# Two blocks of gated features turned by TensorE in the first feed-forward step of a decoder trunk

## The chip, the cores and the metric

The kernel runs on one core of one Trainium2 chip. The metric is device time in microseconds for one execution, as the median of several runs. A core has five engines with a queue each: TensorE (PE in the rows, its weight loads PEld), VectorE (DVE), ScalarE (ACT), GpSimd (POOL) and SyncE (SP), which here issues nearly all DMA transfers and does nothing else.

## The reference

The reference is a decoder trunk of two layers on 256 tokens of width 1024, in float32. Each layer has a feed-forward half step, a mixing step with two kinds of attention, a second feed-forward half step and a gated input embedding. The change touches only the first feed-forward half step of the first layer:

```
def swiglu(x, w_gate, w_up, w_down):
    return (jax.nn.silu(x @ w_gate) * (x @ w_up)) @ w_down

h = h + 0.5 * swiglu(rms_norm(h, ffn1_norm), ffn1_w_gate, ffn1_w_up, ffn1_w_down)
```

The hidden width is 2816. The product of `silu(gate)` and `up` is called the gated features below. `w_down` contracts over them, so they have to stand with features on the partitions, while the matmuls that make them leave tokens on the partitions. Somewhere between they are turned.

## The kernel before

**Operands in two parts.** Every matmul of weights is done as three (`mm3`, lines 250 to 256): each operand is split into a high half, rounded for TensorE, and a low half that holds the rest. For a weight tile of 128x1024, `Unit.load` (line 141) issues one DMA of 512 KB into `raw` (line 148, on SyncE), then ScalarE makes the high half `wh` (line 152) and VectorE the low half `wl` (line 153). `raw` has 7 buffers and the pair `wh`, `wl` has 8. So each weight tile costs VectorE and ScalarE one pass, beside the matmuls that use it.

**The feed-forward step** (`ffn`, line 531) goes through six blocks of 512 hidden features (the last has 256). An ordinary block runs the gate matmuls `g` and then the up matmuls `u` for two groups of 128 tokens, 48 matmuls each, from eight weight tiles. In a *wide seven* block (`wide_seven`, line 573) the gate and up matmuls of the first half of the contraction are one 2x2 block product by seven multiplications: `Seven.operands_own_first` loads four raw tiles, VectorE forms sums of them (line 188), and seven operand pairs are made (`Seven.parts`, lines 193 and 194). Such a block has fewer matmuls and more work for VectorE. In the first step of the program only block 3 is of this kind; in all other steps blocks 1 and 3 are. Block 0 of the first step runs its gate and up matmuls interleaved while inputs still arrive, and its gating is done only behind the gate matmuls of block 1, when the norm of the input is known.

**Gating and turning.** `gated` (line 534) lets ScalarE make `silu` of `g` (tile `s`, line 536) and then VectorE the gated features `pr` from `u` and `s` (line 540). `Gates.add` (line 495) turns them: VectorE transposes each 32x32 square of `pr` in place (line 502), SyncE writes `pr` to memory as `m` (line 504, 256 KB), four more transfers of 64 KB bring it back in another order as `ft` (line 509), and then `parts` (line 511) splits `ft` into the halves `fh` by ScalarE (line 516) and `fl` by VectorE (line 517). Blocks 1 to 3 need sums of the features as well (`Gates.sums`, lines 469 to 472 and 476 to 481), because the down product is again done by seven multiplications. The columns of the gate and up weights are put into a fitting order on the host (`turned_order`), so that the features come back in the right place.

**The order of the work.** Python emits the instructions, and a planner then orders each engine's queue by the sequence of emission and by when it expects inputs and buffers to be there. Once the program is built, each queue is fixed and runs strictly in its order. `soon(us, f)` and `tick` place pieces of work so many microseconds of estimated TensorE time later in the emission: `back` (the transfers of `ft`) 2.5 us and `parts` 7 or 8 us after `add`. `after(later, earlier)` fixes the order of two instructions on the same engine. PSUM has eight banks, all in one pool.

Of the kernel before, what the change touches and what calls it, by code (L numbers as in the profile page):

```python
# [9 lines left out]
F32 = mybir.dt.float32  # L10
F32R = mybir.dt.float32r
BF16 = mybir.dt.bfloat16
AF = mybir.ActivationFunctionType
ALU = mybir.AluOpType
# [3 lines left out]
P = 128  # L18
# [13 lines left out]
SEVEN = (1, 2, 3)  # L32

BACK, PARTS = 2.5, 7.0


def turned_order(n):


    import numpy as np

    return np.arange(n).reshape(n // P, 4, 32).transpose(1, 0, 2).reshape(-1)


def wide_sevens(first):

    return (3,) if first else (1, 3)
# [15 lines left out]
def trunk(ctx: ExitStack, tc: tile.TileContext, xT, xr, pT, w, gains, fgain, consts, out):  # L65
    nc = tc.nc
# [34 lines left out]
    ident = c_sb[:, 0:P]  # L101
# [12 lines left out]
    def after(later, earlier):  # L114

        tc.add_manual_dep(later.ins, earlier.ins.name, mybir.DependencyInfo(mybir.DependencyClass.NoSync, mybir.DependencyReason.DATA), reason="order")
# [9 lines left out]
    newest_load, newest_wh = [None], [None]  # L126
    fence = [None, None]

    class Unit:


        def __init__(self, nk, cols=None, sub=1, cut=1, again=None):
            self.u = at[0] if again is None else again.u
            at[0] += again is None
            self.cols = cols or UNIT // nk
            self.per = max(1, PIECE // self.cols)
            self.sub, self.cut = sub, cut
            self.parts, self.here = {}, set()
# [97 lines left out]
    def soon(us, f):  # L236
        due.append((pe[0] + us, len(due), f))
# [14 lines left out]
    newest_mm = [None]  # L252
# [8 lines left out]
    def both(x, *ix):  # L261
        return tuple(t[ix] for t in x)
# [32 lines left out]
    def in_runs(x):  # L295

        return x.rearrange("p j (a s) -> p j a s", s=32)
# [134 lines left out]
    class Gates:  # L432


        def __init__(self, tag):
            self.tag, self.f, self.s, self.turned = tag, {}, {}, {}

        def tile(self, i):
            if i not in self.f:
# [12 lines left out]
        def sums(self, i):  # L452

            a, b = self.turned[i, 0], self.turned[i, 1]
            lo, hi = (slice(None), slice(0, 2)), (slice(None), slice(2, 4))
            e = SEVEN.index(i)
            if e == 0:

                self.spare = tuple(x_p.tile([P, KC, T], F32R, tag=f"x{q}", name=f"sx{q}_{self.tag}") for q in "hl")
            if e < 2:  # L460
                homes = [[q[:, 4 * e + k].rearrange("p (a b) -> p a b", a=2) for q in self.spare] for k in range(4)]
            else:

                homes = [[q[:, 2 + k].rearrange("p (a b) -> p a b", a=2) for q in self.tile(NBLK - 1)] for k in range(2)]
                homes += [[q[:, 0:2, P:T] for q in self.tile(c)] for c in SEVEN[:2]]
            two = [wt("w3", f"sum{k}_{self.tag}_{i}") for k in range(2)]
            ss = [two[k // 2][:, k % 2].rearrange("p (a b) -> p a b", a=2) for k in range(4)]
            s1, s2, s3, s4 = (in_runs(s) for s in ss)
            nc.vector.tensor_tensor(s1, b[lo], b[hi], ALU.subtract)
            nc.vector.tensor_tensor(s2, s1, a[lo], ALU.subtract)  # L470
            nc.vector.tensor_tensor(s3, a[lo], b[lo], ALU.subtract)
            nc.vector.tensor_tensor(s4, s2, a[hi], ALU.add)
            if e < 2:
                for k in range(2):
                    sh, sl = (q[:, 4 * e + 2 * k : 4 * e + 2 * k + 2] for q in self.spare)
                    nc.scalar.activation(sh, two[k], AF.Copy)
                    nc.vector.tensor_tensor(sl, two[k], sh.bitcast(F32), ALU.subtract)
            else:
                for k, (sh, sl) in zip(ss, homes):
                    nc.scalar.activation(sh, k, AF.Copy)  # L480
                    nc.vector.tensor_tensor(sl, k, sh.bitcast(F32), ALU.subtract)
            self.s[i] = homes
# [13 lines left out]
        def add(self, i, t, pr, more):  # L496


            f = self.block(i)
            n = 4 if i < NBLK - 1 else 2  # L500
            name = f"{self.tag}_{i}{t}"
            nc.vector.transpose(pr, pr)
            m = mem_p.tile([P, 4, n * 32], F32, tag="turn", name=f"m_{name}")
            nc.sync.dma_start(m, pr.rearrange("p (q r) -> p q r", q=4))
            a = wt("w2", f"ft_{name}", 4, n * 32)

            def back():
                for q in range(4):
                    nc.sync.dma_start(a[32 * q : 32 * q + 32], m[:, q].rearrange("(a f) r -> f a r", a=4))

            def parts():
                self.turned[i, t] = v = a.rearrange("p a (j s) -> p j a s", j=n)

                ks = slice(2 if i in SEVEN and t else 0, n)
                fh, fl = (in_runs(q) for q in both(f, slice(None), ks, slice(t * P, (t + 1) * P)))
                after(nc.scalar.activation(fh, v[:, ks], AF.Copy), newest_wh[0])
                nc.vector.tensor_tensor(fl, v[:, ks], fh.bitcast(F32), ALU.subtract)
                if i in SEVEN and t:
                    self.sums(i)

            soon(BACK, back)
            soon(PARTS + t, parts)

    def seven_mm(banks, x_of, ops, first, last):

# [3 lines left out]
                mm3(banks[p], x_of(p, j), (wh[:, c], wl[:, c]), first(p) and j == 0, last(p) and j == 1, skip_group_check=True)  # L529

    def ffn(x, n, tag, gcol, between=None, feed=None):
        gates = Gates(tag)

        def gated(i, t, g, u, m=512):
            s = flat("w0", f"s_{tag}_{i}{t}")[:, :m]
# [71 lines left out]
        for i in range(NBLK):  # L607
# [18 lines left out]
            if i == 0 and feed:  # L626
# [7 lines left out]
                first = [g, u]  # L634
# [38 lines left out]
        p = {2: d[0][0], 3: d[0][1], 4: d[1][0]}  # L673
# [16 lines left out]
        u, v, a, b = (flat(f"w{k}", f"{m}7_{tag}") for k, m in enumerate("uvab"))  # L690
# [376 lines left out]
    n = Norm("in")  # L1067
# [18 lines left out]
    for L in range(DEPTH):  # L1086
        g0 = L * G_LAYER
        x, n = ffn(x, n, f"a{L}", g0 + G_MIX, feed=None if L else start)
        x, n = mix(x, n, L, g0)
# [12 lines left out]
def _weights(i):  # L1102

    import numpy as np

    def cols(w, m):

        return w[:, m].reshape(-1, P, len(m)).transpose(1, 0, 2).reshape(P, -1)

    ar = np.arange  # L1110
    units = []
    for L in range(DEPTH):

        def wide(w, m):

            units.extend(cols(w[k : k + 512], m) for k in range(0, DM, 512))

        def ffn(n):
            wg, wu, wd = (i[f"{n}_w_{s}"][L] for s in ("gate", "up", "down"))
            for j in range(NBLK - 1):  # L1120
                m = 512 * j + turned_order(512)
                if j in wide_sevens(L == 0 and n == "ffn1"):
                    units.extend(np.concatenate([cols(v[k : k + 256], m) for v in (wg, wu)], axis=1) for k in (0, 256))
                    units.extend(cols(v[512:], m) for v in (wg, wu))
                    continue
                wide(wg, m)
                wide(wu, m)
            m = DFF - 256 + turned_order(256)
            wide(np.concatenate([wg[:, m], wu[:, m]], axis=1), ar(512))

            def down(b):
                units.extend(cols(wd[k : k + 256], ar(DM)) for k in range(512 * b, min(512 * b + 512, DFF), 256))

            def seven(b):
                for k in (512 * b, 512 * b + 256):
                    units.append(np.concatenate([cols(wd[k : k + 256], ar(c, c + 512)) for c in (0, 512)], axis=1))

            down(0)
            down(NBLK - 1)
            for b in SEVEN:  # L1140
                seven(b)
            down(4)

        ffn("ffn1")
        wi = i["w_in"][L]
        rot = np.r_[32:64, 0:32]
        wide(wi, ar(1024, 1536))
        for m in (0, 512, 256, 768):
            units.append(cols(wi, ar(m, m + 256)))
        units.append(cols(wi, ar(1536, 1792)))  # L1150
        units.append(cols(wi, np.r_[1792:1920, 1920:1984, 1920 + rot]))
        uq = i["w_uq"][L]
        nope = np.concatenate([192 * h + ar(128) for h in range(4)])
        rope = np.concatenate([192 * h + 128 + ar(64) for h in range(4)])
        rotd = np.concatenate([192 * h + 128 + rot for h in range(4)])
        units.append(cols(uq, np.r_[nope, rope, rotd]))
        ukv = i["w_ukv"][L]
        kn = np.concatenate([256 * h + ar(128) for h in range(4)])
        u = np.zeros((P, UNIT), ukv.dtype)
        u[:, :1024] = cols(ukv, np.r_[kn, kn + 128])  # L1160
        units.append(u)
        for k in range(0, DM, 256):
            units.append(cols(i["w_out"][L][k : k + 256], ar(DM)))
        ffn("ffn2")
        units.append(cols(i["w_ple_proj"][L], ar(DM)))
        for m in range(0, DM, 512):
            wide(i["w_ple_gate"][L], ar(m, m + 512))
    return np.stack(units)
# [55 lines left out]
```

## Time and profile before

| | us |
|---|---|
| median of 3 runs | 1006.04 |
| lowest and highest run | 1004.79, 1007.29 |
| profiled execution | 1003.63 |
| its span, first to last instruction | 1001.8 |
| TensorE busy in the span | 981.6 |
| VectorE busy | 861.9 |
| ScalarE busy | 635.7 |

The profile is of one execution. Times in it count from the first instruction. A busy share is an average over a millisecond; where a change works on a short stretch, the table of that stretch counts, above all the number of matmuls that started in it. A matmul's recorded length overlaps with the next, so the spacing of starts tells the rate. A wait names the instruction that came last.

### The profile page before, as it was taken

The page shows a single profiled execution, that of the slowest core. Times are in us where ns is not written, and L with a number is a line of the kernel's source. Part 1 is how long each engine was busy: PE and PEld are TensorE (multiplying, and loading weights), DVE is VectorE, ACT ScalarE, POOL GpSimd, SP SyncE. Part 2 cuts the span into 40 slices and gives each one's busy share as a digit, 9 for nine tenths or more (in the row PEclk, how much of TensorE's full clock was granted, in tenths as well). Part 3 has the DMA queues.
Part 4 walks back from the last instruction along what each step waited for, and adds up shares of the span by engine and source line. Part 5 has one row for each costly group of instructions (what it writes and reads, how often), then busy time and mean ns, then how long its engine had stood idle before and what let it go on. Part 6 is the DMA issues. An engine that isn't in the chain of part 4 may idle for free.

```text
span 1001.8 us, 14087 instructions
## 1 busy us (share of the span) xinstructions
PE 981.6 (98%) x4888; PEld 824.2 (82%) x4888; DVE 861.9 (86%) x1218; ACT 635.7 (63%) x974; POOL 12.4 (1%) x13
## 2 busy tenths in 40 slices
PE   9998999999999999999999999999999999999996
PEld 7875888899888888887788888888998888888875
DVE  6689999967679999799998998899676799989995
ACT  6746656848566566567676556567766755756664
POOL 0000000000100000000000000002000000000000
PEclk9999999999999999999999999999999999999999
DMA  8876875675233778685737686676733357776651
GB/s 302 302 252 202 302 231 188 230 257 175 98 127 108 268 224 274 197 259 194 262 105 264 229 272 213 212 249 210 274 106 106 126 174 251 267 240 204 222 187 43
DMA packets 88055, 210.50 MB, mean 210 GB/s; under 512 B 14000, under 2 KB 35632, under 8 KB 87984
## 3 DMA queue, kind: packets, MB, share of 16 engines
q1 hardware_dynamic: 87552, 209.03, 62.1%
q8 instruction: 38, 0.62, 0.2%
q10 hardware_dynamic: 432, 0.57, 0.2%
q14 instruction: 33, 0.27, 0.1%
HBM read 196.98 MB, written 12.58 MB: 209 GB/s over the span
## 4 chain that ended last, share of the span: by engine, by line
PE 86%; DVE 5%; DMA 4%; ACT 3%; issue 1%; SPq 0%; ACTq 0%; DVEq 0%
DMA raw<-in_w 4%; PE p_b L256 3%; PE g_a L256 3%; PE p_b L257 3%; PE g_a L258 3%; PE g_a L257 3%; PE g_b L257 3%; PE g_b L258 3%; PE g_b L256 3%; PE p_b L258 3%; PE d_a L257 3%; PE d_a L258 3%; PE d_a L256 3%; PE p_a L257 3%; PE p_a L258 3%; PE p_a L256 2%
## 5 line engine op out<-in xcount | busy, mean ns | idle before, releaser
L153 DVE TENSOR_TENSOR wl<-raw,wh 128x1024 fp32r<-128x1024 f32 (+1 forms) x278 | 321.0, 1187 | 49.5 <-ACT wh L152 48.1
L152 ACT ACTIVATE wh<-raw 128x1024 fp32r<-128x1024 f32 (+1 forms) x278 | 278.5, 1031 | 103.2 <-DMA raw<-in_w 47.4
L193 ACT ACTIVATE wh<-raw 128x1024 fp32r<-128x1024 f32 x133 | 139.0, 1058 | 130.0 <-DVE raw L188 98.9
L194 DVE TENSOR_TENSOR wl<-raw,wh 128x1024 fp32r<-128x1024 f32 x133 | 159.4, 1216 | 11.1 <-ACT wh L193 10.4
L188 DVE TENSOR_TENSOR raw<-raw,raw 128x1024 f32<-128x1024 f32 x76 | 92.6, 1220 | 4.5 <-DMA raw<-in_w 2.4
L256 PE MATMUL d_a<-wh,fh_a 128*128 128x512 f32 x108 | 42.3, 391 | 0.0
L258 PE MATMUL d_b<-wh,fl_b 128*128 128x512 f32 x108 | 42.2, 391 | 0.0
L256 PE MATMUL d_b<-wh,fh_b 128*128 128x512 f32 x108 | 42.2, 391 | 0.0
L258 PE MATMUL d_a<-wh,fl_a 128*128 128x512 f32 x108 | 42.1, 390 | 0.0
L257 PE MATMUL d_b<-wl,fh_b 128*128 128x512 f32 x108 | 42.1, 389 | 0.0
L257 PE MATMUL d_a<-wl,fh_a 128*128 128x512 f32 x108 | 42.0, 389 | 0.0
L256 PE MATMUL g_a<-wh,x0h 128*128 128x512 f32 x80 | 31.1, 390 | 0.3 <-ACT x0h L305 0.3
L257 PE MATMUL g_a<-wl,x0h 128*128 128x512 f32 x80 | 31.0, 389 | 0.0
L258 PE MATMUL g_a<-wh,x0l 128*128 128x512 f32 x80 | 31.0, 389 | 0.0
L257 PE MATMUL u_a<-wl,x0h 128*128 128x512 f32 x64 | 25.2, 394 | 0.5 <-DVE wl L153 0.5
L256 PE MATMUL g_b<-wh,x_mix0h 128*128 128x512 f32 x64 | 25.1, 392 | 0.0
L256 PE MATMUL g_b<-wh,x_mix1h 128*128 128x512 f32 x64 | 25.1, 392 | 0.0
L256 PE MATMUL g_a<-wh,xe0h 128*128 128x512 f32 x64 | 25.0, 391 | 0.0
L258 PE MATMUL u_a<-wh,x0l 128*128 128x512 f32 x64 | 25.0, 390 | 0.0
L258 PE MATMUL g_a<-wh,xe0l 128*128 128x512 f32 x64 | 24.9, 390 | 0.0
L257 PE MATMUL g_a<-wl,xe0h 128*128 128x512 f32 x64 | 24.9, 389 | 0.0
L258 PE MATMUL g_b<-wh,x_mix0l 128*128 128x512 f32 x64 | 24.9, 389 | 0.0
(552 smaller groups left out, 2683.9 us busy)
## 6 DMA issues: line engine op xcount, KB each, us to landing
raw<-in_w SPq DMA_DIRECT2D x338, 512.0 KB, 5.1
m_a<-pr_a SPq DMA_DIRECT2D x20, 256.0 KB, 2.1
ft_a<-m_a SPq DMA_DIRECT2D x80, 64.0 KB, 2.7
m_b<-pr_b SPq DMA_DIRECT2D x20, 256.0 KB, 2.3
ft_b<-m_b SPq DMA_DIRECT2D x80, 64.0 KB, 2.9
raw<-in_w SPq DMA_DIRECT2D x16, 256.0 KB, 4.4
xin<-in_xT SPq DMA_DIRECT2D x4, 256.0 KB, 4.7
h<-in_xr SPq DMA_DIRECT2D x2, 512.0 KB, 8.0
```

Source lines behind the costliest of these rows:

```text
L152: nc.scalar.activation(wh[:, a], r[:, a], AF.Copy),
L153: nc.vector.tensor_tensor(wl[:, a], r[:, a], wh[:, a].bitcast(F32), ALU.subtract),
L188: nc.vector.tensor_tensor(self.raw[o], self.raw[a], self.raw[b], op)
L193: newest_wh[0] = nc.scalar.activation(wh, r, AF.Copy)
L194: nc.vector.tensor_tensor(wl, r, wh.bitcast(F32), ALU.subtract)
L256: nc.tensor.matmul(o, ah, bh, start=start, stop=False, **kw)
L257: nc.tensor.matmul(o, ah, bl, start=False, stop=False, **kw)
L258: newest_mm[0] = nc.tensor.matmul(o, al, bh, start=False, stop=stop, **kw)
```

## The change

In the first feed-forward step blocks 0 and 1 no longer pass through VectorE's transposes and memory. TensorE turns each 128x128 square of `pr` with the identity into a PSUM bank, four squares for each block and group of tokens, and `parts` reads the bank. As an instruction here takes one operand from PSUM where two would be needed, `sums` first copies one quarter of `b` by ScalarE. `soon` places the transposes: for block 1, 1.3 and 2.2 us of estimated TensorE time behind its gating, for block 0 another 4.5 us later. The weight columns of these two blocks keep their natural order. Blocks 2 to 5 of the step, and all other steps, stay as they are. For them `after` is called behind `parts` in place of within it.

```
+def moved(first, i):
+    return not first or i > 1
...
-        def __init__(self, tag):
-            self.tag, self.f, self.s, self.turned = tag, {}, {}, {}
+        def __init__(self, tag, first):
+            self.tag, self.first, self.f, self.s, self.turned = tag, first, {}, {}, {}
...
-            nc.vector.tensor_tensor(s1, b[lo], b[hi], ALU.subtract)
+            blo = b[lo]
+            if not moved(self.first, i):
+                blo = s3
+                nc.scalar.copy(s3, b[lo])
+            nc.vector.tensor_tensor(s1, blo, b[hi], ALU.subtract)
             nc.vector.tensor_tensor(s2, s1, a[lo], ALU.subtract)
-            nc.vector.tensor_tensor(s3, a[lo], b[lo], ALU.subtract)
+            nc.vector.tensor_tensor(s3, a[lo], blo, ALU.subtract)
             nc.vector.tensor_tensor(s4, s2, a[hi], ALU.add)
...
             name = f"{self.tag}_{i}{t}"
+
+            def parts(v):
+                self.turned[i, t] = v
+                ks = slice(2 if i in SEVEN and t else 0, n)
+                fh, fl = (in_runs(q) for q in both(f, slice(None), ks, slice(t * P, (t + 1) * P)))
+                h1 = nc.scalar.activation(fh, v[:, ks], AF.Copy)
+                nc.vector.tensor_tensor(fl, v[:, ks], fh.bitcast(F32), ALU.subtract)
+                if i in SEVEN and t:
+                    self.sums(i)
+                return h1
+
+            if not moved(self.first, i):
+                def go():
+                    a = bank(f"ft_{name}")[:, : n * P]
+                    behind = newest_mm[0]
+                    for j in range(n):
+                        after(nc.tensor.transpose(a[:, j * P : (j + 1) * P], pr[:, j * P : (j + 1) * P], ident), behind)
+                    parts(in_runs(a.rearrange("p (a b) -> p a b", a=n)))
+
+                soon(1.3 + 0.9 * t + more, go)
+                return
             nc.vector.transpose(pr, pr)
             m = mem_p.tile([P, 4, n * 32], F32, tag="turn", name=f"m_{name}")
             nc.sync.dma_start(m, pr.rearrange("p (q r) -> p q r", q=4))
...
             soon(BACK, back)
-            soon(PARTS + t, parts)
+            soon(PARTS + t, lambda: after(parts(a.rearrange("p a (j s) -> p j a s", j=n)), newest_wh[0]))
...
-        gates = Gates(tag)
+        gates = Gates(tag, feed is not None)
...
+                first = L == 0 and n == "ffn1"
-                m = 512 * j + turned_order(512)
+                m = 512 * j + (turned_order(512) if moved(first, j) else ar(512))
```

## Rows read from the trace of the kernel before

**Rows 1.** The page: TensorE's row of the forty slices, busy tenths of 25 us each.
```profile
PE   9998999999999999999999999999999999999996
```

**Rows 2.** The table by stretches. Columns: stretch in us, its length, then busy us and the number of instructions of PE, PEld, DVE, ACT and POOL, the granted clock of TensorE as a share of full speed, the DMA share and GB/s. The last stretch lies in the second feed-forward step.
```profile
40.00:60.00 20.00, 20.00 (x90) 16.57 (x89) 12.12 (x14) 7.85 (x9) 0.00 (x0) 1.00 0.67 206
60.00:80.00 20.00, 16.97 (x66) 12.38 (x64) 19.16 (x28) 11.65 (x17) 0.00 (x0) 0.91 0.78 281
80.00:100.00 20.00, 16.90 (x69) 12.75 (x70) 19.90 (x25) 14.20 (x17) 0.00 (x0) 1.00 0.65 208
100.00:120.00 20.00, 20.00 (x89) 16.55 (x89) 17.61 (x24) 12.50 (x17) 0.00 (x0) 1.00 0.89 294
310.00:330.00 20.00, 20.00 (x90) 16.56 (x89) 19.97 (x23) 13.51 (x16) 0.00 (x0) 1.00 0.39 130
```

**Rows 3.** The waits of TensorE in 60:95, each with its total in us, the number of times and the longest; the longest three totals.
```profile
PE p_a L257 <- DVE wl L194: 3.8, 3, 2.0
PE p_a L256 <- ACT wh L193: 1.6, 2, 1.1
PE u_a L257 <- DVE wl L153: 0.5, 1, 0.5
```

**Rows 4.** The timeline of SyncE's issues: start, time of the group of issues, line, what is moved, and how many.
```profile
22.84 5.32 SPq L148 DMA_DIRECT2D raw<-in_w  x5
37.46 0.92 SPq L504 DMA_DIRECT2D m_a<-pr_a  x2
...
39.52 4.15 SPq L509 DMA_DIRECT2D ft_a<-m_a  x8
43.77 1.32 SPq L148 DMA_DIRECT2D raw<-in_w  x3
51.94 1.14 SPq L504 DMA_DIRECT2D m_a<-pr_a  x2
53.19 0.38 SPq L148 DMA_DIRECT2D raw<-in_w  x1
54.02 5.59 SPq L509 DMA_DIRECT2D ft_a<-m_a  x8
```

**Rows 5.** Waits again, in the same form: SyncE's in 28:76, ScalarE's and VectorE's in 36:66.
```profile
SPq L504 <- DVE pr_a L502: 21.6, 5, 8.4
...
ACT wh L152 <- DMA raw<-in_w: 11.6, 4, 8.4
...
DVE wl L153 <- ACT wh L152: 4.6, 1, 4.6
DVE pr_a L540 <- PE u_a L258: 3.0, 1, 3.0
...
DVE wl L153 <- PE u_a L258: 0.8, 1, 0.8
```

**Rows 6.** The timeline of VectorE in 28:95: start, time, line and operation, how many, and in brackets the idle time before and what ended it.
```profile
36.73 1.29 DVE L502 STREAM_TRANSPOSE pr_a<-pr_a 128x512 f32<-128x512 f32 x2
...
49.26 1.43 DVE L540 SCALAR_TENSOR_TENSOR pr_a<-u_a,hr_in,s_a 128x512 f32<-128x512 f32 x2 [2.97 <-PE u_a L258]
...
60.49 1.23 DVE L153 TENSOR_TENSOR wl<-raw,wh 128x1024 fp32r<-128x1024 f32 x1 [4.60 <-ACT wh L152]
...
65.90 2.35 DVE L153 TENSOR_TENSOR wl<-raw,wh 128x1024 fp32r<-128x1024 f32 x2
...
75.19 1.18 DVE L194 TENSOR_TENSOR wl<-raw,wh 128x1024 fp32r<-128x1024 f32 x1
```

**Rows 7.** Where the seven products start on TensorE, first in the first step (tile p_a), then in the second (tile p_b), with count, shortest, median and longest ns, and the first and last start; and between them the table by stretches for line 194 alone, over the 35.6 us ahead of each start: stretch, length, busy us and number of VectorE's instructions on that line, granted clock, DMA share, GB/s.
```profile
L256 PE MATMUL p_a<-wh,x0h x17: 389/389/502, 72.3 to 99.2; 128*128 128x512 f32 x17
...
36.70:72.30 35.60, 1.22 (x1) 1.00 0.75 249
284.70:320.30 35.60, 6.01 (x5) 1.00 0.31 100
...
L256 PE MATMUL p_b<-wh,x_mix0h x36: 389/389/496, 320.7 to 382.0; 128*128 128x512 f32 x36
```

**Rows 8.** The timeline of TensorE in 185:193, where transposes of h stand between matmuls, and the same transposes as a group of the tile xt_a (shortest, median and longest ns, first and last start).
```profile
185.97 0.39 PE L258 MATMUL d_a<-wh,fl_a 128*128 128x512 f32 x1
186.20 0.60 PE L371 MATMUL xt_a<-c_sb,h 128*128 128x128 f32 x4
186.56 0.48 PE L256 MATMUL d_a<-wh,fh_a 128*128 128x512 f32 x1
186.87 0.40 PE L257 MATMUL d_a<-wl,fh_a 128*128 128x512 f32 x1
...
L371 PE MATMUL xt_a<-c_sb,h x32: 270/272/273, 186.2 to 683.3; 128*128 128x128 f32 x32
```

**Rows 9.** Single operations by their sources: VectorE with one operand from a PSUM bank (p_a), ScalarE's copy from such a bank, and VectorE from SBUF (ft_a).
```profile
L587 DVE TENSOR_TENSOR ch_a<-ch_a,p_a x1: 678/678/678, 84.0 to 84.0; 128x512 f32<-128x512 f32 x1
L584 ACT COPY ch_a<-p_a x1: 586/586/586, 73.9 to 73.9; 128x512 f32<-128x512 f32 x1
...
L517 DVE TENSOR_TENSOR fl_a<-ft_a,fh_a x6: 416/682/684, 45.6 to 87.1; 128x512 fp32r<-128x512 f32 x4, 128x256 fp32r<-128x256 f32 x2
```

**Rows 10.** The chain of work that ended last, in 0:140: start, time, what. Two matmuls: the first of u of block 1, and the first that used the low half of the tile behind the seven products.
```profile
38.76 0.45 PE u_a L256 x2
...
91.77 0.50 PE p_a L257
```

More of the change, by code (lines that the diff above doesn't have):

```diff
@@ L509, in back @@
                     nc.sync.dma_start(a[32 * q : 32 * q + 32], m[:, q].rearrange("(a f) r -> f a r", a=4))
[L511 to L519, printed above, removed]
             soon(BACK, back)
-            soon(PARTS + t, parts)
+            soon(PARTS + t, lambda: after(parts(a.rearrange("p a (j s) -> p j a s", j=n)), newest_wh[0]))
     def seven_mm(banks, x_of, ops, first, last):
@@ L1120, in ffn @@
             for j in range(NBLK - 1):
-                m = 512 * j + turned_order(512)
-                if j in wide_sevens(L == 0 and n == "ffn1"):
+                first = L == 0 and n == "ffn1"
+                m = 512 * j + (turned_order(512) if moved(first, j) else ar(512))
+                if j in wide_sevens(first):
                     units.extend(np.concatenate([cols(v[k : k + 256], m) for v in (wg, wu)], axis=1) for k in (0, 256))
```

## The prediction

> **What bounds the kernel now.** I read the page first: TensorE is busy for 98% of the span, and its row of slices (25 us each) is full but for the fourth digit and the last [rows 1]. So a change of this size can gain only where TensorE stands still, and elsewhere whatever it adds to TensorE is paid. The table by stretches shows where it stands still: 89 or 90 matmuls start in a full stretch of 20 us, but 66 in 60:80 and 69 in 80:100 [rows 2]. That is 24 + 21 = 45 matmuls too few at 20/90 = 0.222 us each, 10.0 us lost. The waits of TensorE in that stretch name 5.9 us of it, by wl (the low halves that VectorE makes) and wh (the high halves of ScalarE) of the first wide seven product [rows 3]; the granted clock of 0.91 in 60:80 is (1 - 0.91) x 20 = 1.8 us more, at the lower level of 1.2 GHz in place of 2.4, after TensorE had stood still [rows 2]; the remaining 2.3 us are slow restarts behind those waits and shorter waits. So the 10.0 us have one cause: VectorE is late with the operands of block 3.
>
> Why is it late? VectorE is 19.2 and 19.9 us busy in 60:80 and 80:100, but only 12.1 in 40:60 [rows 2]. The idle time that it lacks later lies there: 4.6 us for a wh, 3.0 us for the end of u and 0.8 us more [rows 5, 6]. The wh in turn waited for a raw weight tile, 8.4 us the longest [rows 5]. And the raw tile was late because its issue stood on SyncE behind the turning of the features: SyncE issued five loads by 28.2, then nothing until m of block 0 at 37.46; eight ft transfers from 39.52 took 4.15 us of its time; after three loads it stood still again from 45.1 to 51.94 for m of block 1; the next ft group took 5.59 us, and loads flowed again at 59.6 [rows 4]. SyncE's wait for VectorE's transposes is 21.6 us in this stretch [rows 5].
>
> **The change part by part.** *Removed, VectorE:* two pairs of transposes of 128x512, 1.29 us a pair, 2.6 us [rows 6]. Both lie before the stretch in which VectorE has no pause, so they count as lead.
>
> *Removed, SyncE and memory:* four m transfers (0.92 + 1.14 us of issue) and sixteen ft transfers (4.15 + 5.59 us), 11.8 us of issue time, and with them SyncE's stops at 28.2 and 45.1 [rows 4]. What holds a load then is only its buffer. A raw tile has seven buffers, a pair wh/wl eight; the pair of tile n is free when TensorE has used tile n - 8. A tile of an ordinary block serves 12 matmuls, 2.7 us: u of block 1 starts at 38.8 [rows 10], so its four tiles give their pairs back at about 41.5, 44.2, 46.9 and 49.7. Of the four tiles of u of block 2, which are next in turn for them, the second became wl at 60.49 and the last two from 65.90 [rows 6]. The pairs permit them 16 to 19 us earlier, and the loads, once SyncE is free, permit it too.
>
> *A page speaks against this step.* The Trainium skill, DMA: Bandwidth & Descriptors, section Issuing engines are not separate DMA queues, says that the time in which a sequencer starts a DMA is usually small beside the DMA itself. The trace differs here: eight issues hold SyncE for 4.15 to 5.59 us [rows 4]. By the page freeing SyncE would be worth next to nothing; that is rival A.
>
> *Added, TensorE:* 16 transposes of 128x128, in four groups of four. The trace has the same form of work between the same matmuls: from the matmul at 185.97 to that at 186.87 is 0.90 us with one matmul and one group between them, where two spacings of 0.227 would be 0.45 [rows 8]. So a group costs 0.45 us, 1.8 us in all, and all of it is on the path, since TensorE is full until 66. Bounds: nothing, if a group falls into a pause, up to 16 x 0.272 = 4.4 us, if each costs its recorded length [rows 8]. I take 1.8, which is measured between neighbours as here.
>
> The Trainium skill, VectorE: DVE Perf Modes, section The three transpose paths, gives TensorE 390 ns and VectorE 311 ns for a 128x128 transpose; with 16 x 0.39 = 6.2 us the sum below would be -2.5 us. The row's 0.45 us for four decides against it.
>
> *Added, order on TensorE:* the transposes of block 1 stand two and four tile steps (1.4 and 2.7 us) into the next block's matmuls and wait there for pr. Queued behind them is every later matmul. VectorE waited for the end of u, began that pr at 49.26, and had both within 1.43 us [rows 6], by 50.7; the transposes are due at about 51.9 and 53.2 (38.8 and 10.9 for 48 matmuls, 49.7, plus the first two groups' 0.9, plus 1.4 and 2.7). So the wait is nothing if VectorE is free then, and 1.2 us for each subtraction that stands before pr. For block 0 pr was ready near 36.8 and its transposes, 5.8 us behind 38.8, are due at about 44.6, no wait. I take 0 and keep 2.3 us (three subtractions less the 1.2 us in hand) as the upper bound.
>
> *Moved to PSUM:* the high and low halves and the sums read a bank in place of SBUF. VectorE's 128x512 subtraction with one operand in PSUM is 0.678 us, from SBUF 0.682 [rows 9]: nothing either way. The added ScalarE copy of 128x256 is bounded by 0 and the 0.59 us of a 128x512 copy out of PSUM [rows 9]; ScalarE is busy for 7.9 of 20 us in 40:60 [rows 2], which hides it. If that cover were gone it would hold the first sum for 0.6 us, once. The banks of block 1 stay taken until its sums are made; that is well before block 3 wants four banks at about 73, as u of block 2 and these two make four of eight.
>
> *What is late next.* From 36.73 to the first wl of block 3's upper half (TensorE goes on with it at 91.77 [rows 10]) are 55.0 us; VectorE was idle for 8.9 of them (4.6 + 3.0 + 0.8, and some half a microsecond of short pauses) [rows 5, 6], so 46.1 us of work, less 2.6 = 43.5. If all stalls go, TensorE needs that wl at 91.77 - 10.0 + 1.8 = 83.6, 46.9 us behind 36.73. So VectorE may idle 3.4 us on the way. The pauses that the change doesn't touch, for u and the short ones, are 3.0 + 0.8 + 0.5 = 4.3. That leaves about 0.9 us of stall; I take 1.3, one subtraction late. The second feed-forward step shows the state to be reached: five wl of its first wide seven product are made in the 35.6 us before TensorE starts on it at 320.7 [rows 7], and TensorE starts its full 90 matmuls in 310:330 [rows 2]. In the first step one was made by then, at 72.3 [rows 7], and the next came at 75.19 [rows 6].
>
> *Sum:* -10.0 + 1.8 + 1.3 = -6.9 us, rounded to -7.0. The profiled execution took 1003.63 us (span 1001.8 and 1.8 around it), so it would take 996.6. The median of the runs is 2.4 us above it; the same difference on the median gives 999.0. From 100 us on TensorE is full again, so what it gains it keeps.
>
> **The rivals.** *A, only VectorE's own 2.6 us count.* The loads are not what starves VectorE, the buffers are; then VectorE stays without a pause from 60 on and ends 2.6 us earlier, TensorE's groups vanish in its waits, and the time is 1003.4. For it: 19.2 and 19.9 us busy [rows 2]. Against: its 4.6 us pause ended with a load that was issued only at 53 [rows 4 to 6].
>
> *B, TensorE pays in full.* The transposes don't overlap with their neighbours: 4.4 us, so -10.0 + 4.4 + 1.3 = -4.3 in all, 1001.7. Against it is the 0.45 us of a group [rows 8]. By the price of the Trainium skill's page on VectorE it would be 1003.5.
>
> *C, slower: TensorE's queue waits for pr.* The queue orders are made by a planner when the program is built, and VectorE's will be another one. If it puts block 2's subtractions, for which loads now come early, ahead of pr of block 1, TensorE stops at the transposes (decided from the point at which VectorE reaches pr later than 51.2), 2.3 us, and if the same order leaves the operands of block 3 as late as now, nothing is regained: +1.8 + 2.3 = +4.1, 1010.1. Against: VectorE stood ready 3.0 us before u was done [rows 5].
>
> *D, half.* The new order keeps VectorE in front of waits for TensorE for another 2 to 4 us; the stall shrinks to 3.3 to 5.3 us: -3.0 to -5.0, 1001.0 to 1003.0.
>
> **How the numbers follow.** Forecast (996.0 to 1001.0): 0.62. D: 0.15. A: 0.13. C: 0.07. B: 0.03. The time is the forecast's, 999.0. The range begins at 996.0 (-10.0: transposes in pauses, no stall left) and ends at 1003.5, which takes in D, B and A's value; C and A's upper half are left out. About 0.3%, 3.0 us, is what a measurement of this kernel can tell from no change. Faster by more, below 1003.0: forecast, D and most of B, 0.79. Within: A and the rest of B, 0.14. Slower: C, 0.07.
>
> **What would show it.** In the profile after: no 8 us pause of SyncE before m in 28:52 and no ft issues there; VectorE's pauses in 40:60 under 4 us in place of 8; at least four wl of the first wide seven product before TensorE starts on it; 85 or more matmuls in each stretch of 20 us from 60 to 100, and a granted clock of 1.00 there; four groups of transposes at 0.45 us each. It is wrong if TensorE waits for pr at a transpose, if VectorE is idle as long as before (then loads were not the cause), or if the stall merely moves behind 92.

## The result, and the profile after

The changed kernel takes 997.17 us, the median of 4 runs (996.09 to 997.45), beside 1006.08 us for the kernel before on the same chip (4 runs, 1004.79 to 1007.29). The ratio is 0.9910 with a 95% interval of 0.9893 to 0.9927, so 7.3 to 10.8 us of 1006.08. The forecast was 999.0, with a range of 996.0 to 1003.5.

In the kernel after, lines 148 to 153 of before are 154 to 159, lines 188 and 193 to 194 are 194 and 199 to 200, the three matmuls of `mm3` (256 to 258 in the rows of before) are 262 to 264, `pr` is made in line 564, and the new transposes are line 531. The table by stretches of the kernel after, which answers to [rows 2]:

```profile
40.00:60.00 20.00, 20.00 (x98) 16.59 (x97) 19.34 (x23) 14.22 (x18) 0.00 (x0) 1.00 0.86 312
60.00:80.00 20.00, 20.00 (x90) 16.58 (x89) 19.96 (x26) 14.04 (x17) 0.00 (x0) 1.00 0.42 138
80.00:100.00 20.00, 20.00 (x90) 16.57 (x89) 19.30 (x27) 12.16 (x16) 0.00 (x0) 1.00 0.84 291
```

The 66 and 69 matmuls have become 90 and 90, the granted clock is 1.00, and VectorE does in 40:60 the work that it lacked: 19.3 us in place of 12.1, 0.7 us of pauses where the forecast asked for under 4. (The 98 instructions of TensorE in 40:60 are 82 matmuls and the 16 transposes.) Of the waits in [rows 3] none is left: TensorE's list of waits for 28:100 is empty.

How much that is worth is read from a point behind the stretch. The first matmul of the down product (tile d_a in 100:185, group rows: count, shortest, median and longest ns, first and last start) of the kernel before,

```profile
L256 PE MATMUL d_a<-wh,fh_a x47: 389/389/389, 134.5 to 184.8; 128*128 128x512 f32 x47
```

and of the kernel after:

```profile
L262 PE MATMUL d_a<-wh,fh_a x54: 389/389/477, 126.4 to 182.4; 128*128 128x512 f32 x54
```

It starts 8.1 us earlier. That start is the yardstick for most of what follows, since nothing that comes later than the stretch is in it. What comes ahead of the stretch is in it: a second execution of the changed kernel starts the down product at 127.4, and there the `u` of block 1 already starts 1.0 us later (39.88 beside 38.83). So differences of less than about 1 us in this number need a look at where they begin.

SyncE's timeline after, which answers to [rows 4]:

```profile
23.44 20.80 SPq L154 DMA_DIRECT2D raw<-in_w  x12
45.05 4.33 SPq L191 DMA_DIRECT2D raw<-in_w  x4
50.79 22.79 SPq L154 DMA_DIRECT2D raw<-in_w  x7
75.19 0.92 SPq L538 DMA_DIRECT2D m_a<-pr_a  x2
```

Twelve loads go out where five did, and the four raw tiles of the seven product (line 191) are issued at 45.05. What a load waits for is now mostly a buffer, which comes free when a low half has been made. SyncE's two longest waits in 28:76, and all of VectorE's in 36:66, beside [rows 5]:

```profile
SPq L154 <- DVE wl L200: 17.3, 4, 15.1
SPq L154 <- DVE wl L159: 13.0, 8, 5.4
```
```profile
DVE pr_a L564 <- ACT s_a L560: 1.5, 1, 1.5
DVE wl L159 <- ACT wh L158: 0.5, 1, 0.5
DVE wl L200 <- ACT wh L199: 0.2, 1, 0.2
```

VectorE's timeline, beside [rows 6], shows `pr` of block 1 with no pause ahead of it, and behind it the last two low halves of block 2, which in the kernel before came at 65.90:

```profile
50.68 1.40 DVE L564 SCALAR_TENSOR_TENSOR pr_a<-u_a,hr_in,s_a 128x512 f32<-128x512 f32 x2
52.00 2.35 DVE L159 TENSOR_TENSOR wl<-raw,wh 128x1024 fp32r<-128x1024 f32 x2
```

Where the seven product starts, and the low halves made for it by then, beside [rows 7]:

```profile
L262 PE MATMUL p_a<-wh,x0h x18: 389/389/389, 73.3 to 92.4; 128*128 128x512 f32 x18
...
L200 DVE TENSOR_TENSOR wl<-raw,wh x7: 1218/1219/1224, 55.1 to 72.0; 128x1024 fp32r<-128x1024 f32 x7
```

All seven are begun before TensorE starts on them at 73.3; in the kernel before it was one. The new transposes between matmuls, beside [rows 8]:

```profile
44.72 0.39 PE L264 MATMUL u_a<-wh,x0l 128*128 128x512 f32 x1
44.95 0.60 PE L531 MATMUL ft_a<-c_sb,pr_a 128*128 128x128 f32 x4
45.30 0.48 PE L262 MATMUL u_a<-wh,x0h 128*128 128x512 f32 x1
45.62 0.40 PE L263 MATMUL u_a<-wl,x0h 128*128 128x512 f32 x1
...
52.00 0.60 PE L531 MATMUL ft_a<-c_sb,pr_a 128*128 128x128 f32 x4
...
53.82 0.60 PE L531 MATMUL ft_a<-c_sb,pr_a 128*128 128x128 f32 x4
```

From 44.72 to 45.62 are 0.90 us, with one matmul and four transposes between: 0.45 us a group, as in [rows 8]. The groups of block 1 stand at 52.00 and 53.82 and don't wait.

### The profile page after: what moved, and what is told of

Its sections match the earlier page's. It is cut to its first block, busy times and chain, and to the rows that moved or that the text cites. A ratio compares the mean times of both kernels' runs of the same rounds, so it can differ in the third digit from the quotient of the medians.

```text
span 995.5 us, 14077 instructions
## 1 busy us (share of the span) xinstructions
PE 980.2 (98%) x4904; PEld 825.0 (83%) x4904; DVE 860.1 (86%) x1214; ACT 636.5 (64%) x975; POOL 7.8 (1%) x13
## 4 chain that ended last, share of the span: by engine, by line
PE 87%; DVE 5%; ACT 3%; DMA 3%; issue 1%; SPq 0%; DVEq 0%; ACTq 0%
PE p_b L262 3%; PE p_b L263 3%; PE p_b L264 3%; PE g_b L262 3%; PE g_b L264 3%; PE g_b L263 3%; PE g_a L263 3%; PE g_a L264 3%; PE g_a L262 3%; PE u_a L263 2%; PE u_a L264 2%; PE u_a L262 2%; PE p_a L262 2%; PE p_a L264 2%; PE p_a L263 2%; PE u_b L262 2%
## 5 line engine op out<-in xcount | busy, mean ns | idle before, releaser
L262 PE MATMUL u_a<-wh,x0h 128*128 128x512 f32 x64 | 24.9, 392 | 0.0
```

The source lines that it names most:

```text
L262: nc.tensor.matmul(o, ah, bh, start=start, stop=False, **kw)
```

## The experiments

Two theories were to be told apart. The forecast's own: SyncE's stops for `m` and `ft` make the loads late, and nothing else matters (the first chain). Its rival: the features' trip through memory is a second chain. The queues of VectorE and ScalarE have a fixed order, so whatever stands behind `fh`, `fl` and the sums of block 1 comes late with them, and among it are the sums of x that the seven product needs. All ratios are against the kernel before on the same chip; the columns on the right are the first matmul of the down product and the matmuls in 60:80 and 80:100. Code is shown without the lines that tell `Gates` that it is in the first step (`self.first`), as in the change.

| run | median us | ratio (95%) | down product | 60:80, 80:100 |
|---|---|---|---|---|
| before | 1006.08 | 1 | 134.5 | 66, 69 |
| after | 997.17 | 0.9910 (0.9893 to 0.9927) | 126.4 | 90, 90 |
| e9_unread: stops stay, trip's wait gone | 1005.77 | 0.9988 (0.9978 to 0.9997) | 134.4 | 72, 68 |
| e3_pool: stops gone, trip stays | 1006.81 | 0.9993 (0.9979 to 1.0007) | 131.8 | 65, 84 |
| e6_pool_xs_late: the same, halves and sums moved | 1006.72 | 1.0001 (0.9990 to 1.0013) | 133.0 | 76, 65 |
| e10_no_trip: both gone | 998.81 | 0.9918 (0.9902 to 0.9934) | 125.1 | 89, 90 |
| e7_xs: both stay, sums of x early | 1005.26 | 0.9987 (0.9978 to 0.9996) | 134.5 | 69, 67 |
| e4_no_dve: no VectorE transposes | 1005.72 | 0.9988 (0.9977 to 0.9999) | 134.9 | 66, 69 |
| e5_thrice: each transpose three times | 999.37 | 0.9925 (0.9911 to 0.9940) | 130.1 | 90, 90 |
| e1_block0: only block 0 by TensorE | 999.98 | 0.9926 (0.9910 to 0.9943) | 129.9 | 71, 90 |
| e2_block1: only block 1 by TensorE | 999.64 | 0.9934 (0.9920 to 0.9949) | 128.3 | 90, 83 |
| e1_xs: block 0, and sums of x early | 996.39 | 0.9901 (0.9885 to 0.9918) | 125.6 | 90, 90 |
| e1_xs_again | 996.19 | 0.9895 (0.9879 to 0.9912) | 125.9 | 89, 87 |
| after_again | 997.64 | 0.9908 (0.9893 to 0.9923) | 127.4 | 90, 90 |

**SyncE freed, the trip kept (e3_pool).** The kernel before, with the transfers of blocks 0 and 1 issued by GpSimd:

```
...
-            nc.sync.dma_start(m, ...)
+            eng = nc.gpsimd if self.first and i < 2 else nc.sync
+            eng.dma_start(m, ...)
...
-                    nc.sync.dma_start(a[...], m[...])
+                    eng.dma_start(a[...], m[...])
...
```

> The kernel before, but the m and ft transfers of blocks 0 and 1 of the first step are issued by GpSimd's queue in place of SyncE's. VectorE keeps its 2.6 us of transposes, TensorE gets no transposes. Theory (SyncE standing behind the turning made the weight tiles late): SyncE's stops in 28:52 go, weight tiles are issued as their buffers come free, at least four wl of the first wide seven product stand before TensorE gets there, and of the 10.0 us that TensorE lost in 60:100 at most 3 remain; time 996 to 1000, and 996 would be as fast as the changed kernel or faster, as no transposes stand on TensorE. Rival A (VectorE's own 2.6 us): VectorE's work is as before, so the loss stays between 8 and 10 us and the time at 1004 to 1006. A third possibility: transfers of GpSimd's queue land later than SyncE's, so that the halves of the features hold VectorE; then the loss is between.

SyncE issued twelve loads from 23.35 on, and the four raw tiles of the seven product from 45.34, as in the kernel after, though over 8.0 us in place of 4.3. The time stayed where it was, against the 996 to 1000 of the first theory. SyncE's timeline, the table by stretches (columns as in rows 2), and then TensorE's waits in 60:95 and one of ScalarE's in 36:66:

```profile
23.35 21.19 SPq L148 DMA_DIRECT2D raw<-in_w  x12
45.34 8.03 SPq L185 DMA_DIRECT2D raw<-in_w  x4
```
```profile
40.00:60.00 20.00, 20.00 (x89) 16.52 (x88) 16.49 (x18) 11.09 (x13) 5.49 (x10) 1.00 0.97 334
60.00:80.00 20.00, 15.78 (x65) 12.70 (x64) 17.91 (x26) 12.82 (x17) 4.39 (x8) 0.89 0.41 130
```
```profile
PE p_a L256 <- ACT xsh_a L563: 4.2, 1, 4.2
```
```profile
ACT fh_a L517 <- DMA ft_a<-m_a: 5.0, 1, 5.0
```

and three lines of VectorE's timeline:

```profile
50.84 0.69 DVE L518 TENSOR_TENSOR fl_a<-ft_a,fh_a 128x512 fp32r<-128x512 f32 x1 [3.25 <-ACT fh_a L517]
...
67.48 0.69 DVE L518 TENSOR_TENSOR fl_a<-ft_a,fh_a 128x512 fp32r<-128x512 f32 x1 [1.99 <-ACT fh_a L517]
...
74.50 0.41 DVE L556 TENSOR_TENSOR xsum_a<-xf_a 128x256 f32<-128x256 f32 x1
```

The loads fill the DMA engines (share 0.97 in 40:60), `ft` lands late, VectorE stands 3.25 us for the halves of block 0 and 1.99 us for those of block 1, and the sums of x behind them begin at 74.50. TensorE, which wanted them at 73.4, stands 4.2 us and then runs at the lower clock level for a while (granted 0.89 in the stretch). No wait for wl or wh of the seven product is left, though the exchange moves as many bytes as before: it was not its traffic that made the loads late. So of 10.0 us the down product got 2.7, and 7.3 stayed although the first chain was gone, here with a trip that GpSimd issued and that took longer than SyncE's (last section). The 2.7 were lost later: matmul by matmul, the lead over the kernel before falls from 2.75 us at 190 to 0.89 at 220, where the planner had put the queues in another order, and is gone by 500. Freeing SyncE is not enough.

**The trip lengthened in the order (e6_pool_xs_late).** As e3_pool, with the sums of x ahead of block 2, and the halves 5 us later in the emission, so that VectorE would not stand for them.

```
...
-            soon(PARTS + t, parts)
+            soon((12.0 if self.first and i < 2 else PARTS) + t, parts)
...
+            if i == 2 and feed is not None:
+                x_sums()
...
```

> The kernel before with m and ft of blocks 0 and 1 on GpSimd's queue, the sums of x emitted ahead of block 2, and the halves of the features of these two blocks emitted 5 us later, so that VectorE does not come to them before the data. If the memory trip hurts only because some queue stands and waits for it (SyncE for pr, or VectorE for ft), this kernel has no stall left and no transposes on TensorE: 995.5 to 998. If the trip itself is too long in this stretch, in which weight tiles take the whole of the DMA engines: 1001 to 1006.

It moved the wait once more. In 28:76 ScalarE waited 10.3 us in three pieces for `ft`. TensorE waited 5.3 us, until 82.38, for a copy of ScalarE (`ch`), which stood in ScalarE's queue behind three high halves made from 78.91 on, and the down product gained 1.5 us. That the halves of the features come later in the order doesn't help: the trip was longer still, and what is behind them is late too.

**The sums of x alone (e7_xs).** The kernel before with the two lines at `i == 2` only.

> The kernel before with one change of order: the four sums of x and their halves (1.4 and 1.3 us of VectorE, 1.3 us of ScalarE) are emitted ahead of block 2 in place of ahead of block 3. Nothing is added or removed. So far: taking 2.6 us of transposes away ahead of VectorE's dense stretch gave about nothing, freeing SyncE alone about nothing. If work inside the dense stretch (60 to 92) is what counts, moving 2.6 us of it out into the pauses of 40:60 gives 2 to 2.6 us: 1003.5 to 1004.5. If the raw tiles, which SyncE still issues late, set the end of that stretch: 1005.5 to 1007.

Next to nothing: by the ratio 0.4 to 2.2 us, the down product starts at 134.5 as before, and TensorE waits for wl and wh of the seven product (2.8 and 2.6 us). With SyncE's stops in place the raw tiles are late, whatever stands ahead in VectorE's queue.

**The stops kept, the trip's wait taken out (e9_unread).** The counterpart of e3_pool: SyncE issues every `m` and `ft` as before, but the halves and sums are made from `pr`.

```
...
-                self.turned[i, t] = v = a.rearrange("p a (j s) -> p j a s", j=n)
+                v = in_runs(pr.rearrange("p (a b) -> p a b", a=n)) if self.first and i < 2 else a.rearrange("p a (j s) -> p j a s", j=n)
+                self.turned[i, t] = v
...
```

> The kernel before with one edit: in blocks 0 and 1 of the first step all transfers of m and ft are issued by SyncE as before, but nothing reads what they bring back; the halves and sums are made straight from pr in SBUF, whose squares are turned only 32x32 (the turning across squares is left out, so the features of these blocks are wrong). So SyncE's stops stay and the wait for the trip through memory is gone. If each of the two chains is enough to hold TensorE: SyncE still stops for about 8 us ahead of m, raw tiles come late as before, 8 to 10.5 us are lost by TensorE in 28:100, the down product starts at 133 to 135, and the time is within 2 us of the kernel before. If the trip's wait alone was the cause: under 3 us lost, the down product starts near 125, and the time is 7 to 10 us below the kernel before.

The first theory's chain by itself holds TensorE as long as before. The table by stretches, SyncE's timeline, and TensorE's waits in 60:95:

```profile
60.00:80.00 20.00, 16.71 (x72) 12.97 (x71) 16.75 (x20) 10.78 (x13) 0.00 (x0) 1.00 0.78 284
80.00:100.00 20.00, 17.59 (x68) 13.36 (x67) 19.90 (x26) 13.78 (x18) 0.00 (x0) 0.91 0.67 226
```
```profile
23.54 5.32 SPq L148 DMA_DIRECT2D raw<-in_w  x5
38.16 0.92 SPq L504 DMA_DIRECT2D m_a<-pr_a  x2
...
45.74 1.32 SPq L148 DMA_DIRECT2D raw<-in_w  x3
52.05 1.13 SPq L504 DMA_DIRECT2D m_a<-pr_a  x2
...
60.87 2.05 SPq L185 DMA_DIRECT2D raw<-in_w  x4
```
```profile
PE p_a L257 <- DVE wl L194: 2.9, 2, 1.7
PE p_a L256 <- ACT wh L193: 2.4, 3, 0.9
```

The raw tiles of the seven product are issued at 60.87 in place of 45.05, and the waits have the form of [rows 3]. Whether the wait for `pr` (8.3 us the longest) or the 5.3 and 5.7 us of issuing `ft` weighs more is not told apart by this run. The exchange's traffic runs here too; that it doesn't make the loads late is what e3_pool shows.

**Both taken out (e10_no_trip).** As e9_unread, but `m` and `ft` of the two blocks are not issued.

> As the last, but the transfers of m and ft of blocks 0 and 1 are not issued at all (the turning across squares is left out). SyncE is free and nothing waits for memory; VectorE still transposes its squares, TensorE gets no transposes. If the two chains together are the whole cause: no stall left in 28:100 (under 1 us), the down product starts at 124.3 to 125.3 (134.5 less the 10 us lost), 1.3 to 2 us earlier than in the changed kernel, and the time is 995 to 996.5. If VectorE's 2.6 us of transposes count once the loads flow: 1 to 2.6 us lost in 60:100, the down product starts at 125.5 to 127, time 997 to 998.5.

The table by stretches, and the first matmul of the down product:

```profile
60.00:80.00 20.00, 20.00 (x89) 16.55 (x89) 19.91 (x24) 13.79 (x16) 0.00 (x0) 1.00 0.39 131
80.00:100.00 20.00, 20.00 (x90) 16.56 (x89) 19.97 (x27) 12.33 (x15) 0.00 (x0) 1.00 0.85 299
```
```profile
L256 PE MATMUL d_a<-wh,fh_a x54: 389/389/395, 125.1 to 181.1; 128*128 128x512 f32 x54
```

No wait of TensorE is left in 60:95, though VectorE still transposes its squares, and the down product starts at 125.1: 9.4 us before the kernel before, 1.3 before the kernel after. The kernel after pays 1.8 us of transposes; this one has a wait of 0.4 us for a wl at 39.8. So the two chains are the whole stall. The time itself was a miss, 998.81 in place of 995 to 996.5. TensorE's timeline shows where it went:

```profile
183.51 0.60 PE L371 MATMUL xt_a<-c_sb,h 128*128 128x128 f32 x4
184.33 0.50 PE L256 MATMUL v<-wh,x_a0h 128*128 128x512 f32 x1 [0.22 <-ACT x_a0h L305]
```

From the first matmul of v (181.80) to the first of q (190.52) are 8.7 us, 6.5 in the kernel after (183.06 to 189.56): the planner put the transposes of h elsewhere, and TensorE waits for their results in small pieces. Of these 2.2 us 1.9 stay lost: matmul by matmul, the lead over the kernel before falls from 9.4 us at 190 to 7.6 at 220. It is the loss of e3_pool in the same place, so it goes with another order of the queues and not with the two chains.

**VectorE's transposes (e4_no_dve).** Rival A's 2.6 us, taken out alone.

```
...
-            nc.vector.transpose(pr, pr)
+            if not (self.first and i < 2):
+                nc.vector.transpose(pr, pr)
...
```

> The kernel before without VectorE's transposes of blocks 0 and 1 of the first step: the 32x32 squares are left unturned there, the m and ft transfers on SyncE stay. Theory: SyncE still stands for pr at m and still spends 11.8 us on these issues, so VectorE's pauses in 40:60 stay near 8 us; VectorE has 2.6 us less to do, of which the stretch behind 60 sees at most that; loss of TensorE in 60:100 7 to 9.5 us, time 1003.5 to 1005.5. Rival A: the 2.6 us come off the end of VectorE's stretch in full, 1003.4, and freeing SyncE (the other kernel of this call) gives nothing.

The same 66 and 69 matmuls, the down product at 134.9. By the ratio the run is 0.1 to 2.3 us faster, which rules out the 2.6 us of rival A. What is taken from VectorE's work becomes longer pauses: 5.5 us for wh in place of 4.6, and 1.5 us for `fh` that was not there.

**The price of a transpose (e5_thrice).** The kernel after, with `for j in [*range(n)] * 3`.

> The changed kernel with each of the 16 transposes on TensorE done three times into the same bank. My term of 0.45 us for a group of four: 32 more transposes cost 8 x 0.45 = 3.6 us, so 1000.8 against 997.2 of the changed kernel, if TensorE is full throughout (theory). By the recorded length (rival B, 0.272 us each) 8.7 us more, 1005.9. If the groups fell into pauses of TensorE: nothing, 997.2. If the matmul behind a group pays once for the group and not for each transpose, the longer group costs less than in proportion, 1.5 to 3 us.

TensorE's timeline at the first group:

```profile
44.96 0.39 PE L264 MATMUL u_a<-wh,x0l 128*128 128x512 f32 x1
45.19 1.47 PE L531 MATMUL ft_a<-c_sb,pr_a 128*128 128x128 f32 x12
46.42 0.47 PE L262 MATMUL u_a<-wh,x0h 128*128 128x512 f32 x1
```

Twelve take 46.42 - 45.19 = 1.23 us, four took 45.30 - 44.95 = 0.35: eight more cost 0.88, 0.11 us each, and 32 more 3.5. The down product starts 3.7 us later, and the `u` of block 1 starts in the same place (38.81 beside 38.83). The median is only 2.2 us above the kernel after, below the 1000.8 expected; the kernel after loses 1.9 us between 623 and 720 us (below), this one 0.5. Rival B's recorded length would have been 32 x 0.272 = 8.7 us. The Trainium skill (VectorE: DVE Perf Modes, The three transpose paths) gives 390 ns, for bf16 where these are float32; by that it would have been an estimated 12.5 us. For transposes in a row between matmuls the trace doesn't agree.

**Each block alone (e1_block0, e2_block1).** The kernel after with `i > 0` or `i != 1` in `moved`.

> The changed kernel with block 0 alone turned by TensorE; block 1 goes through VectorE and memory as before. Theory: of SyncE's two stops the first (28 to 37.5) goes, the second (near 45 to 52) and the 5.6 us of ft issues stay, so the tiles of u of block 2 come a few us late still; TensorE pays 0.9 us; loss in 60:100 2 to 6 us, time 998 to 1003. If the stop for block 0 was the cause, nearly no loss, 997. If the stop for block 1 was the cause, loss 8 to 10 us, 1005 to 1007.

> The changed kernel with block 1 alone turned by TensorE; block 0 goes through VectorE and memory as before. SyncE's first stop (28 to 37.5) and 4.2 us of ft issues stay, the second stop and 5.6 us of issues go; TensorE pays 0.9 us. By the two stops together as the cause: loss 2 to 5 us of 10, 999 to 1003. If block 1's way (SyncE's second stop, its late features) is all that counts: no loss, 997. If block 0's: 1005 to 1007.

Either one brings more than half: the down product starts 4.6 and 6.2 us earlier. With block 0 alone one wait of TensorE is left in 60:95:

```profile
PE p_a L262 <- ACT xsh_a L586: 2.7, 1, 2.7
```

It is for the sums of x, the second chain. VectorE and ScalarE don't stand still for block 1's features there: VectorE works without a pause in 50:80 and begins these sums at 71.06 in place of 62.65, since its queue has them behind block 1's halves and sums. It is thus the place in the order that costs here; in e3_pool it was waiting as well. With block 1 alone ScalarE still waits 6.2 us for raw tiles in 28:76, TensorE 0.9 us for wh, and 83 matmuls start in 80:100 (the first chain, by what these waits suggest).

**Block 0 by TensorE and the sums of x early (e1_xs, e1_xs_again, after_again).** If these sums are all that block 1's trip holds up, they can be moved in place of turning block 1.

> Block 0 alone turned by TensorE, as in the earlier run, and the sums of x emitted ahead of block 2. In that run the largest wait left was TensorE's for a half of the sums of x (2.7 us, and a spell at the lower clock behind it), because these sums stand on VectorE and in their buffer behind the sums of block 1, which wait for its features from memory. If that is the way by which block 1's turning holds TensorE, the wait goes: 1006.5 - 10 + 0.9 + 0 to 1.5, 997.5 to 999. If the weight tiles behind SyncE's second stop hold it, the wait only changes its name: 999.5 to 1001.

> The same kernel as the one with only block 0 turned by TensorE and the sums of x made ahead of block 2, beside the changed kernel on one chip. If only two groups of transposes are paid and no stall is left, 0.5 to 1.2 us below the changed kernel in this comparison: 995.8 to 996.8.

> The changed kernel itself, beside the others: 997.0 to 998.0, down product from about 126.4, no stall of TensorE in 28:100. It tells how far the stretch of 640 to 690, where its first profile lost 2.2 us, differs from execution to execution: if it is by chance, this profile loses less there.

But for one wait of 0.3 us in the second execution the stall is gone with two groups of transposes in place of four, the down product at 125.6 and 125.9. The 996.39 of the first is below the 997.5 to 999 expected. SyncE still issues `m` and `ft` of block 1 here (in the first execution at 52.63 and 56.09), behind twelve loads and three of the four raw tiles of the seven product: its second stop by itself holds nothing up. This version lies below the changed kernel by 0.8 us (from another chip) and by 1.5 us (on the same one); the means of all eight runs of each are 996.4 and 997.3. The intervals of the two ratios overlap, so a gain of about the 0.9 us of two groups is likely rather than settled.

## Why the prediction was right

**What bounds the kernel, 10.0 us.** Right. The 10.0 us are gone with the waits of [rows 3], and 8.1 us at the down product are 10.0 less the 1.8 paid, to a tenth; e10_no_trip, which pays none, has 9.4 with a wait of 0.4 left. A count of matmuls in a stretch gave the sum at once, while the named waits gave only 5.9 us of it.

**One cause, SyncE's stops.** Right as a sufficient cause (e9_unread: it alone keeps TensorE as late as before), wrong as the only one. Behind it stood a second chain, the features' trip and the sums of x in its wake: 7.3 of the 10.0 us stayed with it in e3_pool, and the down product of e1_block0 is 4.3 us behind that of e1_xs. The step that passed over it is the one on what is late next: it counted VectorE's work and pauses, and gave the halves no arrival time of their own. The sum didn't suffer, by luck: the change happens to remove both chains.

**Removed, VectorE, 2.6 us as lead.** Worth nothing at the down product alone (e4_no_dve), and with the loads flowing not needed either (e10_no_trip keeps these transposes and has no stall in 60:95). Rival A falls. The rule of the Trainium skill (DMA: Bandwidth & Descriptors, Issuing engines are not separate DMA queues), that the time to start a DMA is usually small beside the DMA itself, was taken to speak for it. Issue by issue the trace agrees with that rule, against what the prediction says: an issue of `ft` took 0.5 to 0.7 us [rows 4], its transfer a median of 3.9 us to land. What held the loads was eight such issues in a row and an issue that waited up to 8.3 us for `pr` (e9_unread), with every load of the same queue behind it.

**Loads 16 to 19 us earlier.** Over-estimated in size: the second and the last two low halves of block 2 came at 49.55 and 52.00 in place of 60.49 and 65.90, 10.9 and 13.9 us earlier. It was enough.

**Added, 1.8 us.** Right to a tenth: 0.45 us a group, and e5_thrice confirms 0.11 us a transpose. Rival B falls.

**Order on TensorE, 0 us.** Right: the forecast had the transposes of block 1 at 51.9 and 53.2, they ran at 52.00 and 53.82, and `pr` was there. Rival C's premise was there, its price was not: the planner did put low halves ahead of `pr`, which slid from 49.26 to 50.68, but that is within the 51.2 that the forecast gave as the point from which it decides. Rival D, a stall that only shrinks, falls with the full stretches.

**To PSUM, nothing.** Right: `fl` took 0.68 us as from SBUF [rows 9], and ScalarE's copy 0.37 us, once.

**What is late next, +1.3 us.** The mis-sized term: it measured 0. The forecast let 4.3 us of pauses stand, of which 3.0 were VectorE's wait for u. That pause was not a property of u: in the kernel before VectorE had nothing ahead of `pr` in its queue but to wait, and with tiles at hand earlier the planner put low halves there (the one at 49.55 ends where `pr` begins). It then idled 2.2 us in 36:66, less than the 3.4 us that the same paragraph allows. With 0 in place of 1.3 the sum is -8.2, against 8.1 at the down product; the measured medians differ by 8.9, with an interval of 7.3 to 10.8.

**From 100 us on what is gained is kept.** Only nearly. The profiled executions differ by 6.3 us (1003.63 and 997.31), less than the medians. Against the trace of before, matmul by matmul, the trace after is 7.9 us ahead at 623 us and 6.0 us at 720. The second profile of the changed kernel also loses 2.0 us between these points, the two of e1_xs lose 0.7 us and nothing, and from about 207 us on the orders of all queues are the same in before, after and e1_xs. A part of it is a wait of TensorE for one high half of a weight tile of k (0.8 and 1.0 us in the two profiles of the changed kernel, 0.2 in before and in the second of e1_xs); what makes these stretches differ stays open.

**From the profile to the median, 2.4 us.** Not borne out. The profiled execution of before (1003.63) was quicker than all of its other runs in this study, and the forecast carried the 2.4 us from it to the median over to the changed kernel. There the median (997.17) is 0.1 us below the profiled execution (997.31). The forecast's 996.6 for that execution is 0.7 us off because the 1.3 us that didn't come and the 2.1 us that were lost behind the down product nearly cancel; that the forecast of the time is no more than 1.8 us off is in part such luck.

## What to carry to other kernels

When one engine issues the loads and also an exchange that waits for a result, look for two things in the trace: which loads stand behind that wait, and which work stands behind the exchange's return in the in-order queues that consume it. Where two causes overlap, removing one shows next to nothing in the time (e3_pool and e9_unread gained under 0.15%), so an edit that brings nothing doesn't clear its suspect; it takes the run with both removed (e10_no_trip). And a pause ahead of an instruction is a fixed cost only if nothing else can be put ahead of that instruction in the engine's queue.

## What the runs showed of the hardware

Transposes of 128x128 in float32, recorded at 0.272 us each, follow one another at 0.11 us between matmuls. The trip through memory was slower where the loads ran: 64-KB transfers of `ft` took a median of 3.9 us from issue to landing in 28:76 of the kernel before, where SyncE issued them and no load meanwhile, and 5.4 and 7.0 us in 20:76 of e3_pool and e6_pool_xs_late, where GpSimd issued them (0.55 us an issue) beside loads at a DMA share of 0.97 and 0.92; whether the loads or GpSimd's queue made them slow was not tried. After TensorE's stand of 4.2 us in e3_pool nine spacings of 0.43 us followed in place of 0.227, about 1.8 us lost at the lower level of 1.2 GHz on top of the wait (granted clock 0.89 in 60:80 and 0.94 in 80:100).
